# A two-number constant moves from the first SBUF pool to the last: the tiles in between begin 32 bytes lower

## The chip, the core and the metric

The kernel runs on one NeuronCore of a Trainium2 chip. The metric is the device time of one execution in microseconds (us), taken as the median of several executions. SBUF is the core's on-chip memory: 128 partitions, in each of which a tile takes a run of bytes; an address below is the byte within a partition at which a tile begins. Engines are named as in the profile: PE is TensorE's matmul and PEld its weight load, DVE is VectorE, ACT is ScalarE, POOL is GpSimd, SP is the queue that issues most DMAs.

## The reference

A backbone of two layers over 256 latent tokens and 256 context tokens of width 1024. Cut to what the kernel's time goes into:

```python
for l in range(2):
    m = silu(c) @ w_ada[l] + b_ada[l]               # shift, scale, gate: 9 x 1024, for latent and context
    x = ffn_sublayer(x, m, 0, ff1_gate[l], ff1_up[l], ff1_down[l], ...)   # 1024 -> 2816 -> 1024
    y = hybrid_mixer(modulate(x, m, 1), w_in[l], w_out[l], ...)           # attention, RG-LRU, Fourier
    x = layer_norm(alpha * x + m[5] * y)
    x = ffn_sublayer(x, m, 2, ff2_gate[l], ff2_up[l], ff2_down[l], ...)

def ffn_sublayer(x, m, j, wg, wu, wd, g, b):
    h = x * (1 + m[3*j + 1]) + m[3*j]
    y = 0.5 * (silu(h @ wg) * (h @ wu)) @ wd
    return layer_norm(alpha * x + m[3*j + 2] * y)
```

The context stream leaves out what the last layer doesn't need. All inputs and the output are 32-bit floats.

## The kernel before

Activations lie transposed: 8 chunks of 128 features in the partitions, 512 tokens (256 context, 256 latent) along the free dimension. Every large product is done in three passes for accuracy. A weight unit of 128x1024 floats comes by one DMA from SP into a tile `raw` (`issue`, lines 246 to 257), ACT rounds it to fp32r in `whi` (L274), and DVE or POOL writes the rest, raw minus whi, to `wlo` (`split_lo`, L591). The input is split the same way into `hH` and `hL` (for the down projection `aH` and `aL`), and `mmh` (L391) issues high by high, high by low and low by high, each in pieces of 128 weight columns and 256 tokens. Each such matmul has its own weight load of 128x128 from whi or wlo; hH, hL, aH or aL is what moves through the array. In the profile's rows the moving operand stands first: `gu<-hH,whi` reads hH as moving operand and whi as weights. For the transposes (`ptp<-cs,P`) the tile that is transposed (P) is the one that is loaded as weights, and the identity in `cs` moves.

The modulation products go another way: blocks of w_ada come into `raw` too, and DVE multiplies and adds them into `acc` (L302, L304, L298).

SBUF is shared out by pools, in the order in which they are opened, lines 70 to 77: `const` (one copy of each of its tiles), `wraw` (5 tiles `raw`), `whi` (5), `wlo` (5), `acc` (6), `scr` (13 tiles of 512 floats), `sm`, `dv` (small columns). Within a pool the tiles follow each other in the order of their first use, each rounded up to 32 bytes. In `const` come first `xT`, `hH`, `hL`, `aH`, `aL`, then `cs`, `vT`, `onesD`, `one_c`, `pick`, `scol`, and then `join`, the tile that the change moves: 2 floats in each partition. Behind it in `const` stand `bmean`, `kcol`, `lbd`, `fbd`, `AB` and `mcol`. `join` is written once by a DVE reduction at the start and read as the small moving operand of 40 matmuls (`adat<-join,rows`, L332).

What runs in which order is written out by hand and by lists in the kernel; none of it depends on an address.

Of the kernel before, what the change touches and what calls it, by code (L numbers as in the profile page):

```python
# [11 lines left out]
F32 = mybir.dt.float32  # L12
# [53 lines left out]
def kernel(ctx: ExitStack, tc: tile.TileContext, x, cx, vecs, cst, bias, w_ada,  # L66
# [3 lines left out]
    const = ctx.enter_context(tc.tile_pool(name="const", bufs=1))  # L70
# [6 lines left out]
    dv = ctx.enter_context(tc.tile_pool(name="dv", bufs=2))  # L77
# [19 lines left out]
    one_c = const.tile([128, 1], F32, name="one_c")  # L97
    pick = const.tile([128, 2, 2], F32, name="pick")
    scol = const.tile([128, KD, 2], F32, name="scol")
    join = const.tile([128, 2], F32, name="join")  # L100
    bmean = const.tile([128, 6], F32, name="bmean")
    kcol = const.tile([128, 8], F32, name="kcol")
    lbd = const.tile([128, 8, 128], F32, name="lbd")
# [1307 lines left out]
```

## Time and profile before

| | |
|---|---|
| median of 3 runs | 1831.57 us (1828.18 to 1833.34) |
| the profiled execution | 1830.9 us |
| its span, first to last instruction | 1829.0 us |
| mean granted TensorE clock | 0.983 of full speed |
| PE busy | 1751.4 us, 96% of the span, 14241 matmuls |
| DVE busy | 1224.8 us, 67% |
| ACT busy | 700.6 us, 38% |
| POOL busy | 327.9 us, 18% |
| DMA | 253.33 MB, mean 139 GB/s |

A share of busy time is a mean over the whole span. What decides the time is the chain of work that ended last, which the profile follows back from the last instruction.

### The profile page before, as it was taken

The numbers are of one execution on the slowest core, as the hardware profiler recorded it, in microseconds if no ns is written. First come the engines' busy times: TensorE is split into PE (matmuls) and PEld (weight loads), VectorE is DVE, ScalarE is ACT, GpSimd is POOL, SyncE is SP. The second block draws the span as 40 slices with busy tenths as digits, with TensorE's granted clock in tenths as the row PEclk, the third lists the DMA queues.
The fourth block names the chain that finished last, engine by engine and source line by source line (L and its number), as shares of the span: only waits on it lengthen the run. The fifth ranks groups of instructions, "written<-read, shape, count | busy, mean of one in ns | idle before, by whom it ended". The sixth has DMA issues, their size and how long they took to land.

```text
span 1829.0 us, 33865 instructions
## 1 busy us (share of the span) xinstructions
PE 1751.4 (96%) x14241; PEld 1698.2 (93%) x14241; DVE 1224.8 (67%) x1867; ACT 700.6 (38%) x1119; POOL 327.9 (18%) x258
## 2 busy tenths in 40 slices
PE   7999999999899999999999999999999988979997
PEld 5999999998788999999999999999999868869997
DVE  3799899837586488755664569844643759666555
ACT  2232222225756564312222363222222565555443
POOL 0142122215441061000000140000000545140000
PEclk9999999999999999999999999999999999989998
DMA  7566555532223226544453226555653233266662
GB/s 263 181 195 187 170 167 170 171 95 81 69 59 93 59 82 180 162 139 136 132 157 114 86 81 196 166 171 166 178 169 88 81 93 93 82 192 192 177 190 80
DMA packets 375080, 253.33 MB, mean 139 GB/s; under 512 B 8144, under 2 KB 336336, under 8 KB 374928
## 3 DMA queue, kind: packets, MB, share of 16 engines
q1 hardware_dynamic: 373856, 248.81, 46.3%
q8 instruction: 112, 1.84, 0.4%
q0 software_dynamic: 1072, 2.36, 0.4%
q14 instruction: 40, 0.33, 0.1%
HBM read 250.09 MB, written 1.05 MB: 137 GB/s over the span
## 4 chain that ended last, share of the span: by engine, by line
PE 79%; DVE 15%; ACT 3%; issue 2%; DMA 0%; POOL 0%; SPq 0%; DVEq 0%; ACTq 0%
PE gu L391 42%; PE dn L391 21%; PE head L391 5%; PE pj L391 3%; PE wo L391 2%; DVE acc L304 2%; PE adat L332 1%; DVE ri L903 1%; DVE wlo L591 1%; PE o L1097 1%; DVE xl L870 1%; DVE s L460 1%; DVE xT L718 1%; DVE s L463 1%; PE adap L315 1%
## 5 line engine op out<-in xcount | busy, mean ns | idle before, releaser
L391 PE MATMUL gu<-hH,whi 128*128 128x256 f32 x2336 | 500.1, 283 | 2.0 <-ACT hH L1262 1.8
L391 PE MATMUL gu<-hH,wlo 128*128 128x256 f32 x2336 | 497.4, 282 | 2.1 <-DVE wlo L591 2.1
L391 PE MATMUL gu<-hL,whi 128*128 128x256 f32 x2336 | 497.6, 282 | 1.2 <-DVE hL L591 1.1
L274 ACT CAST whi<-raw 128x1024 fp32r<-128x1024 f32 (+1 forms) x319 | 318.8, 1024 | 284.3 <-PE dn L391 104.8
L591 POOL TENSOR_TENSOR wlo<-raw,whi 128x1024 fp32r<-128x1024 f32 (+2 forms) x106 | 207.7, 1966 | 1191.3 <-ACT whi L274 1153.7
L391 PEld LDWEIGHTS gu<-hH,whi 128*128 128x128 f32 x2336 | 374.1, 190 | 5.9 <-ACT hH L1262 2.6
L391 PEld LDWEIGHTS gu<-hH,wlo 128*128 128x128 f32 x2336 | 373.9, 190 | 2.6 <-DVE wlo L591 2.6
L391 PEld LDWEIGHTS gu<-hL,whi 128*128 128x128 f32 x2336 | 374.1, 190 | 1.7 <-DVE hL L591 1.7
L591 DVE TENSOR_TENSOR wlo<-raw,whi 128x1024 fp32r<-128x1024 f32 (+1 forms) x245 | 295.5, 1209 | 92.8 <-ACT whi L274 89.5
L391 PE MATMUL dn<-aH,whi 128*128 128x256 f32 x1280 | 286.3, 283 | 0.8 <-DVE xT L718 0.8
L391 PE MATMUL dn<-aH,wlo 128*128 128x256 f32 x1280 | 283.6, 281 | 0.0
L391 PE MATMUL dn<-aL,whi 128*128 128x256 f32 x1280 | 283.6, 281 | 0.0
L304 DVE SCALAR_TENSOR_TENSOR acc<-raw,scol,acc 128x512 f32<-128x512 f32 x337 | 275.2, 864 | 1.0
L731 ACT CAST aH<-pr 128x512 fp32r<-128x512 f32 (+1 forms) x88 | 50.0, 568 | 422.9 <-DVE pr L730 422.9
L391 PEld LDWEIGHTS dn<-aH,whi 128*128 128x128 f32 x1280 | 208.7, 189 | 1.4 <-DVE xT L718 1.2
L391 PEld LDWEIGHTS dn<-aH,wlo 128*128 128x128 f32 x1280 | 208.7, 189 | 0.1
L391 PEld LDWEIGHTS dn<-aL,whi 128*128 128x128 f32 x1280 | 208.7, 189 | 0.0
L730 DVE TENSOR_TENSOR pr<-sg,gu 128x512 f32<-128x512 f32 (+1 forms) x84 | 51.5, 614 | 148.7 <-PE gu L391 146.2
L718 DVE SCALAR_TENSOR_TENSOR xT<-dn,gate,xT 128x256 f32<-128x256 f32 x174 | 78.0, 478 | 90.5 <-PE dn L391 90.0
L729 ACT ACTIVATE sg<-gu 128x512 f32<-128x512 f32 (+1 forms) x84 | 45.3, 539 | 115.5 <-PE gu L391 115.3
L391 PE MATMUL pj<-hH,whi 128*128 128x256 f32 x384 | 84.5, 288 | 4.9 <-DVE k L591 2.7
L391 PE MATMUL pj<-hH,wlo 128*128 128x256 f32 x384 | 83.1, 285 | 0.0
(239 smaller groups left out, 2127.7 us busy)
## 6 DMA issues: line engine op xcount, KB each, us to landing
raw<-in_w_ada_dram SPq DMA_DIRECT2D x136, 512.0 KB, 4.6
raw<-in_ff_gate_dram SPq DMA_DIRECT2D x88, 512.0 KB, 4.4
raw<-in_ff_up_dram SPq DMA_DIRECT2D x88, 512.0 KB, 4.8
raw<-in_ff_down_dram SPq DMA_DIRECT2D x64, 448.0 KB, 4.5
raw<-in_w_in_dram SPq DMA_DIRECT2D x36, 512.0 KB, 3.9
raw<-in_ff_down_dram SPq DMA_DIRECT2D x32, 512.0 KB, 4.8
raw<-in_w_out_dram SPq DMA_DIRECT2D x16, 512.0 KB, 4.1
in<-in_w_ada_dram SPq DMA_DIRECT2D x8, 512.0 KB, 6.9
```

Source lines behind the costliest of these rows:

```text
L274: S.copy(h_[:, :n], t[:, :n])
L304: V.scalar_tensor_tensor(out=a[:, st], in0=t[:, kk * 512:(kk + 1) * 512], scalar=sc_, in1=a[:, st], op0=ALU.mult, op1=ALU.add)
L315: PE.matmul(acc[l, b][32 * (k % 4):32 * (k % 4) + 32, :], lhsT=scol_z[:, k, :], rhs=t[:, kk * 512:(kk + 1) * 512], start=(k < 4), stop=(k ...
L332: PE.matmul(tp[:, q * 2:q * 2 + 2], lhsT=a[:, q * 128:(q + 1) * 128], rhs=w, start=True, stop=True)
L391: PE.matmul(o[:, c], lhsT=w, rhs=X[:, k, c], start=first and i == 0, stop=last and i == len(halves) - 1)
L460: (e1 or V).tensor_tensor(out=s1, in0=a, in1=z, op=ALU.add)
L463: (e2 or V).tensor_tensor(out=s2, in0=b, in1=sq, op=ALU.add)
L591: (eng or V).tensor_tensor(out=dst_l, in0=src, in1=dst_h.bitcast(F32), op=ALU.subtract)
L718: V.scalar_tensor_tensor(out=xT[:, j, a:b], in0=ps[:, a:b], scalar=gate[:, st, j:j + 1], in1=xT[:, j, a:b], op0=ALU.mult, op1=ALU.add)
L729: S.activation(out=sg[:, c], in_=gp[:, c], func=AF.Silu)
L730: V.tensor_tensor(out=pr[:, c], in0=sg[:, c], in1=up[:, c], op=ALU.mult)
L731: S.copy(aH[:, m, c], pr[:, c])
```

## The change

One line: `join` is taken from the pool `dv`, the last one, in place of `const`, the first one.

```diff
@@ -97,7 +97,7 @@
     one_c = const.tile([128, 1], F32, name="one_c")
     pick = const.tile([128, 2, 2], F32, name="pick")
     scol = const.tile([128, KD, 2], F32, name="scol")
-    join = const.tile([128, 2], F32, name="join")
+    join = dv.tile([128, 2], F32, tag="join", name="join", bufs=1)
     bmean = const.tile([128, 6], F32, name="bmean")
     kcol = const.tile([128, 8], F32, name="kcol")
     lbd = const.tile([128, 8, 128], F32, name="lbd")
```

No instruction is added, removed or moved: on every engine the two programs have the same instructions in the same order. What differs is where tiles begin, as the two built programs have it:

```
tile            address before (mod 64, mod 256)    address now (mod 64, mod 256)
xT..aL, cs, onesD   16512 .. 105600 (0, 128)        the same
join            106240 (0, 0)                       228032 (0, 192)
lbd             106336 (32, 96)                     106304 (0, 64)
raw, first of 5 114656 (32, 224)                    114624 (0, 192)
whi, first of 5 135136 (32, 224)                    135104 (0, 192)
wlo, first of 5 155616 (32, 224)                    155584 (0, 192)
acc, first of 6 176096 (32, 224)                    176064 (0, 192)
scr, first of 13 200672 (32, 224)                   200640 (0, 192)
dv, from mod on 228064 (32, 224)                    the same
```

The tiles of raw, whi, wlo and acc are 4096 bytes and those of scr 2048 bytes, so all of one pool have the same remainders. Everything from `bmean` to the end of `sm` lies 32 bytes lower; `join` fills the 32 bytes that this leaves ahead of the first tile of `dv`.

## Rows read from the trace of the kernel before

**Rows 1.** The page: busy time and share by engine; granted clock in 40 slices, tenths.

```profile
PE 1751.4 (96%) x14241; PEld 1698.2 (93%) x14241; DVE 1224.8 (67%) x1867; ACT 700.6 (38%) x1119; POOL 327.9 (18%) x258
...
PEclk9999999999999999999999999999999999989998
```

**Rows 2.** The page: the chain that ended last, shares of the span by engine.

```profile
PE 79%; DVE 15%; ACT 3%; issue 2%; DMA 0%; POOL 0%; SPq 0%; DVEq 0%; ACTq 0%
```

**Rows 3.** Groups by line and form, PE and PEld: count | busy us, mean ns | idle before.

```profile
L391 PE MATMUL gu<-hH,whi 128*128 128x256 f32 x2336 | 500.1, 283 | 2.0 <-ACT hH L1262 1.8
...
L391 PEld LDWEIGHTS gu<-hL,whi 128*128 128x128 f32 x2336 | 374.1, 190 | 1.7 <-DVE hL L591 1.7
...
L391 PE MATMUL dn<-aH,whi 128*128 128x256 f32 x1280 | 286.3, 283 | 0.8 <-DVE xT L718 0.8
...
L391 PE MATMUL pj<-hH,whi 128*128 128x256 f32 x384 | 84.5, 288 | 4.9 <-DVE k L591 2.7 <-ACT pt L1066 2.2
...
L391 PE MATMUL head<-hH,whi 128*128 128x256 f32 x256 | 67.2, 295 | 9.2 <-ACT hH L605 8.6 <-ACT hH L603 0.6
...
L391 PE MATMUL wo<-aH,whi 128*128 128x256 f32 x144 | 34.7, 286 | 0.0
```

**Rows 4.** Windows, L391 alone: stretch, us, PE and PEld busy (instructions), clock, DMA, GB/s.

```profile
820.24:876.67 56.43, 56.25 (x480) 56.04 (x478) 1.00 0.46 136
```

**Rows 5.** Timeline, PE, first and last of 16 rows: start, length.

```profile
508.69 0.59 PE L958 MATMUL fy<-cs,fas 128*128 128x256 f32 x2
...
515.17 0.59 PE L959 MATMUL fy<-cs,fas 128*128 128x256 f32 x2
```

**Rows 6.** Groups by line and form, PE and PEld, weights at either remainder.

```profile
L332 PEld LDWEIGHTS adat<-pick,fold 128*128 128x128 f32 x192 | 23.4, 191 | 1.4 <-DVE fold L356 1.1 <-PE dn L391 0.2
...
L1064 PEld LDWEIGHTS ptp<-cs,P 128*128 128x128 f32 x80 | 9.1, 140 | 2.4 <-DVE P L996 2.3
...
L1064 PEld LDWEIGHTS ptp<-cs,xT 128*128 128x128 f32 x48 | 5.4, 140 | 1.6 <-ACT xT L1000 1.0 <-ACT whi L274 0.4
...
L804 PEld LDWEIGHTS fab<-fbd,cs 128*128 128x128 f32 x8 | 1.2, 192 | 0.0
...
L1064 PE MATMUL ptp<-cs,P 128*128 128x128 f32 x80 | 11.4, 274 | 1.8 <-DVE P L996 1.8
...
L1064 PE MATMUL ptp<-cs,xT 128*128 128x128 f32 x48 | 6.7, 275 | 0.7 <-ACT xT L1000 0.7
```

**Rows 7.** Groups by line and form, DVE and ACT, tiles at either remainder.

```profile
L591 DVE TENSOR_TENSOR aL<-pr,aH 128x512 fp32r<-128x512 f32 x66 | 45.0, 685 | 6.3 <-ACT aH L731 6.2
...
L603 ACT CAST hH<-h 128x256 fp32r<-128x256 f32 x63 | 25.6, 406 | 2.0
...
L356 DVE TENSOR_TENSOR fold<-fold 128x512 f32<-128x512 f32 x24 | 16.4, 683 | 0.0
...
L660 ACT CAST whi<-raw 128x256 fp32r<-128x256 f32 x16 | 6.4, 402 | 0.0
```

**Rows 8.** DMA queues in three windows, 1.8:2.69, 12:15, 98.9:102 us: packets, MB, share of 16 engines.

```profile
q1 hardware_dynamic: 389, 0.19, 72.9%
...
q1 hardware_dynamic: 603, 1.17, 104.6%
...
q0 software_dynamic: 143, 0.65, 50.7%
```

**Rows 9.** The chain in order of time: start us, length us, what (one piece).

```profile
3.17 7.05 DMA in<-in_x_dram
```

**Rows 10.** Waits by engine: who waited for whom, us in total, times, longest.

```profile
SPq L254 <- POOL wlo L591: 363.5, 55, 21.4
SPq L254 <- DVE wlo L591: 297.8, 129, 20.1
...
ACT whi L274 <- DMA raw<-in_ff_down_dram: 63.2, 15, 9.1
...
PE gu L391 <- DVE wlo L591: 2.1, 2, 1.6
```

## The prediction

> **What bounds the kernel now.** I read the page first: PE is busy 96% of the span, DVE 67%, ACT 38% and POOL 18%, and the granted clock is at 0.9 of full speed or more, its upper level of 2.4 GHz, in 38 of 40 slices [rows 1]. Then the chain that ended last: PE has 79% of it, DVE 15%, ACT 3%, and transfers round to 0% [rows 2]. The reader is to see that the time is PE's stream of matmuls, with DVE's share where PE waits for normalisation and attention, and that no queue of DMAs sets the pace.
>
> The stream is nearly all of one kind, the three-pass fp32r matmul at L391. Its counts per pass are 2336, 1280, 384, 256 and 144 [rows 3]; three passes of each make 13,200 of the 14,241 matmuls. In a stretch with no gap 480 of them take 56.43 us at a clock of 1.00 [rows 4], so 117.6 ns each; 13,200 at that rate are 1552 us of the 1829.0 us span. Every one of them loads 128x128 weights from whi or wlo, which are tiles that the change shifts, and moves hH, hL, aH or aL, which stay.
>
> **The change part by part.** No instruction comes, goes or moves, so the only thing that can change is how long an instruction or a transfer takes when its tile begins 32 bytes lower: at a multiple of 64 bytes, where it began half-way between two. Each kind has a price from the nearest rows.
>
> *Weight loads and their matmuls.* The trace has the same operation with weights at either place. The transposes of attention load P from a tile 32 bytes off a multiple of 64, and others load from xT, which is on one: 140 ns and 140 ns for the load, 274 and 275 ns for the matmul [rows 6]. The load of `fold` (off) takes 191 ns and that of `cs` in the Fourier product (on) 192 ns [rows 6]. Those are fp32 operations; the fp32r ones read the same 512 bytes from each partition, but they have no row with weights on a multiple of 64, since whi, wlo and the attention's q all lie off one. So the price per fp32r matmul is not shown, only bounded. From above: 256 columns at one per cycle of 2.4 GHz are 106.7 ns (an estimate), and the fp32 passes of fy over 256 columns, 16 rows of two, start every (515.17 - 508.69) / 30 = 0.216 us [rows 5], which is two cycles per column (213.3 ns) and 2 to 3 ns, with weights off a multiple of 64. The fp32r matmul has 117.6 - 106.7 = 10.9 ns over its columns, so if the whole difference between 10.9 and 2 ns were due to the address, the change would give back 8.9 ns x 13,200 = 117 us. From below: nothing excludes a loss, because the moving tiles already begin on a multiple of 64 and now both streams do; the nearest rows, xT loaded while cs moves (both on a multiple of 64) beside P, show 1 ns in 275 [rows 6], which at 13,200 would be 13 us of loss. I take zero: the pairs of rows 6 differ in exactly what the change alters, and the fy rows, whose weights `fas` lie off a multiple of 64, have no more than 3 ns over their columns.
>
> The Trainium skill (TensorE: Matmul & The Clock Gate, section "Back-to-back issue gap") gives columns / 2.4 GHz + 2.5 ns for an isolated warm matmul and says that in a stream both the weight load and the matmul set the spacing; by its first formula 256 columns would be 109.2 ns, by its second statement a longer spacing needs no address. The fy rows agree with the 2.5 ns, the 117.6 ns of rows 4 do not; an ideal spacing would make the sum about 111 us less, and nothing on the page ties the spacing to an address.
>
> *DVE and ACT.* A subtraction with all operands in shifted tiles (fold, 683 ns) takes as long as one with two operands in tiles that stay on a multiple of 64 (aL, 685 ns) [rows 7]; a cast between two shifted tiles takes 402 ns, one from a shifted tile to hH 406 ns [rows 7]. The differences are 0.3% and 1%. On the chain DVE has 15%, or 274 us, and ACT 3%, or 55 us [rows 2]: 0.3% of the one and 1% of the other are 0.8 and 0.5 us, either way. I take zero.
>
> *Transfers into raw, acc and scr.* The share of 16 engines' time divided by the bytes gives the cost of a row of 512 bytes (into scr), of 2048 bytes (into raw) and of 5120 bytes (into cs, on a multiple of 64) [rows 8]: 0.729 x 16 x 0.89 us / 0.19 MB x 512 B = 28.0 ns; 1.046 x 48 us / 1.17 MB x 2048 B = 87.9 ns; 0.507 x 49.6 us / 0.65 MB x 5120 B = 198 ns. The line through the first two (8.0 ns and 0.0390 ns per byte) gives 208 ns for the third, so a row that begins on a multiple of 64 is at most 5% cheaper than the line says, and part of that is the rounding of the MB column. Where would it matter? The chain has one long piece of transfer, the 7.05 us until the inputs are there [rows 9]. Later, the queue waits for DVE and POOL to free tiles, 297.8 and 363.5 us [rows 10], not the other way round; ACT waits for transfers, 63.2 us for the down weights [rows 10], but PE's own wait for wlo adds up to 2.1 us [rows 10], so the five tiles of each pool cover it. 5% of 7.05 + 2.1 us is 0.5 us; without that cover, 5% of the 63.2 us would be 3.2 us. I take zero.
>
> The Trainium skill has a rule that speaks here (DMA: Bandwidth & Descriptors, section "How a descriptor splits into AXI transactions"): a transaction starts at a multiple of 256 bytes, and a descriptor that starts elsewhere pays for the bytes ahead of it, in beats of 32 bytes. It speaks of reads; read for the SBUF side, 512 bytes from remainder 224 are 23 beats, and from 192 they are 22. By it the sum would be some 0.4 us lower (4.3% of 9.2 us), by the line of rows 8 at most 0.5 us. Rows 8 neither need the rule nor exclude it.
>
> **The sum.** 1830.9 us (profiled execution) + 0 = 1830.9 us, which is 0.7 us below the median of the runs shown; the forecast is 1831 us. What a measurement of this kernel can tell from no change is about 0.3%, or 5.5 us, since its three runs lie within 1828.2 to 1833.3 us. Over 13,200 matmuls that is 0.42 ns, one cycle of TensorE's clock for each: below that an effect on PE isn't seen, above it it is.
>
> **The rivals.**
>
> *Faster, by the weight loads.* The surplus of 10.9 ns per fp32r matmul comes in part from weights that begin half-way between two multiples of 64. For it: no fp32r row with other weights exists, and fp32 passes have only 2 ns. Against it: rows 6, and that the surplus may as well belong to fp32r itself. One to two cycles per matmul give 5.5 to 11 us: 1820 to 1825 us. All of it gives 1831 - 117 = 1714 us.
>
> *Slower, by two streams in step.* Weights and moving operand now begin at the same remainder by 64 and are read at the same time, every 117.6 ns; if both then ask for the same part of SBUF in the same cycle, one waits. The place is the L391 stream, the price one cycle or more per matmul, and it decides from 0.42 ns on: 1 ns gives 13 us, 1844 us; one cycle 1836.5 us. Against it: the transposes of xT have both operands in step and take what those of P take [rows 6].
>
> *A transfer gets cheaper and nothing follows.* Rows of 512 bytes into raw go from 28.0 to about 27 ns, DMA is 46% busy in the middle stretch [rows 4] and falls by a couple of hundredths, and the time stays within 1 us of 1831 us, since transfers are off the chain. This is "no change" with another trace.
>
> *The tiles don't shift.* If the 32 bytes were lost in padding, nothing would change at all. The address table excludes it: raw goes from 114656 to 114624.
>
> **How the numbers follow.** No measurable change, 1825.5 to 1836.5 us, has 0.77 (of it 0.12 with cheaper transfers). Faster has 0.14: 0.09 for one to two cycles, 0.05 for more than that. Slower has 0.09: 0.05 up to 1840 us, 0.04 beyond. These are the chances of the three verdicts as well. The range reaches into the small cases on both sides: 1822 to 1838 us holds the 0.77, about 0.05 of the faster and 0.02 of the slower; its ends are 0.7 and 0.5 ns per matmul.
>
> **What the changed kernel's profile would show.** If I am right, 480 matmuls of L391 in a gapless stretch again take 56.2 to 56.7 us; the mean load stays at 190 ns [rows 3]; fold and whi keep 683 and 402 ns within 1%; the three DMA shares stay; and the span is 1824 to 1834 us. If the weight loads gain, the 480 take 0.2 us less for each cycle, in all stretches alike. If the streams collide, they take that much longer. If the transfers gain, the share of q1 for the same number of 512-byte packets falls from 72.9% to about 70% with the span unmoved. What would make the prediction wrong is an address that matters to fp32r alone, at the one place where no row of this trace has a pair.

## The result, and the profile after

The changed kernel takes 1809.14 us (median of 4, 1805.85 to 1810.58) where the kernel before, run beside it, takes 1832.29 us: a ratio of 0.9875, 95% interval 0.9855 to 0.9896. It is 23 us faster; the prediction said no change. The profiled execution took 1805.85 us with a span of 1804.1 us, 24.9 us below the span before.

The page after, with the chain's shares, answers to [rows 1, 2]:

```profile
PE 1722.3 (95%) x14241; PEld 1667.0 (92%) x14241; DVE 1227.6 (68%) x1867; ACT 699.9 (39%) x1119; POOL 324.7 (18%) x258
...
PE 76%; DVE 16%; ACT 4%; issue 3%; DMA 0%; POOL 0%; SPq 0%; DVEq 0%; ACTq 0%
```

With the same 14241 matmuls PE is busy 1751.4 - 1722.3 = 29.1 us less. The span fell by 24.9 us, so some 4 us of that came back as idle time of PE, and the chain's shares of DVE, ACT and issue each grew by a point. The busy time of the other engines moved by 1% at most. The groups by line and form (count | busy us, mean ns of one) answer to [rows 3, 6, 7]:

```profile
L391 PEld LDWEIGHTS gu<-hL,whi 128*128 128x128 f32 x2336 | 370.8, 190 | 1.6 <-DVE hL L591 1.6
...
L591 DVE TENSOR_TENSOR aL<-pr,aH 128x512 fp32r<-128x512 f32 x66 | 45.0, 686 | 6.3 <-ACT aH L731 6.2
...
L603 ACT CAST hH<-h 128x256 fp32r<-128x256 f32 x63 | 25.6, 407 | 2.0
...
L356 DVE TENSOR_TENSOR fold<-fold 128x512 f32<-128x512 f32 x24 | 16.4, 682 | 0.0
...
L660 ACT CAST whi<-raw 128x256 fp32r<-128x256 f32 x16 | 6.4, 402 | 0.0
```

DVE's and ACT's means moved by 1 ns at most, and even the mean length of a weight load stands at 190 ns. The queue q1 between 12 and 15 us, packets, MB, share of 16 engines, answers to the second of [rows 8]; transfers cost what they did:

```profile
q1 hardware_dynamic: 599, 1.16, 104.7%
```

What changed is how far apart PE's matmuls of L391 start. The windows, L391 alone (stretch, us, PE and PEld busy with their counts, clock, DMA, GB/s), the last row being the stretch of [rows 4]:

```profile
189.09:234.42 45.33, 45.33 (x384) 45.12 (x384) 1.00 0.53 155
235.21:257.08 21.87, 21.87 (x192) 21.67 (x192) 1.00 0.58 172
333.76:366.51 32.75, 32.75 (x288) 32.55 (x288) 1.00 0.56 160
...
810.52:867.20 56.68, 56.52 (x480) 56.31 (x479) 1.00 0.45 135
```

All four are without gaps and at a granted clock of 1.00, the level of 2.4 GHz, and yet they fall into two kinds. 45.33/384 and 56.64/480 (the chain below) are 118.0 ns per matmul; 21.87/192 and 32.75/288 are 113.9 and 113.7 ns. A stretch has some 0.11 us that does not depend on its count, so differences are cleaner: (45.33 - 22.72) / 192 = 117.8 ns between two slow stretches, (43.63 - 21.87) / 192 = 113.3 ns between two fast ones. The chain of the changed kernel in order of time (start, length, what), in pieces:

```profile
188.30 0.79 PE adat L332 x8
189.09 45.33 PE gu L391 x384
234.42 0.79 PE adat L332 x8
235.21 21.87 PE gu L391 x192
...
367.29 22.72 PE gu L391 x192
...
441.83 18.62 PE head L391 x158
...
619.28 20.00 PE wo L391 x168
...
810.40 56.64 PE gu L391 x480
...
953.43 43.63 PE gu L391 x384
...
1434.77 18.74 PE head L391 x159
...
1564.43 2.74 PE wo L391 x24
...
1791.70 1.41 DVE bn L524 x4
```

The same pieces in the chain of the kernel before, with one more at the head:

```profile
337.52 34.28 PE gu L391 x288
...
449.15 18.55 PE head L391 x158
...
626.56 19.92 PE wo L391 x168
...
820.06 56.43 PE gu L391 x480
...
964.20 45.68 PE gu L391 x384
...
1454.27 18.89 PE head L391 x159
...
1583.44 2.85 PE wo L391 x24
...
1816.66 1.40 DVE bn L524 x4
```

The lead is therefore 7.3 us at the first `head`, 7.3 at the first `wo`, 9.7 and 10.8 in the feed-forward stretches behind it, 19.5 at the later `head`, 19.0 at its `wo` and 25.0 at the end. From `head` to `wo` runs the mixer, 177.4 us before and 177.5 now in the one layer, 129.2 and 129.7 in the other: nothing is gained there, the lead grows in the feed-forward streams. And not in all of their stretches: the x384 stretch at 953 us took 45.68 us before and takes 43.63 us now, the x480 stretch took 56.43 us and takes 56.64 us.

Over all starts of one L391 matmul to the next in stretches without a gap, the trace of the changed kernel has a mean of 115.72 ns and that of the kernel before 118.11 ns. The difference of 2.39 ns on 13,200 matmuls is 31.5 us of stream; three quarters of it or a little more reached the end.

### The profile page after: what moved, and what is told of

The parts are those of the page before. It is cut to its first block, busy times and chain, and to the rows that moved or that the text cites. A ratio compares the mean times of both kernels' runs of the same rounds, so it can differ in the third digit from the quotient of the medians.

```text
span 1804.1 us, 33865 instructions
## 1 busy us (share of the span) xinstructions
PE 1722.3 (95%) x14241; PEld 1667.0 (92%) x14241; DVE 1227.6 (68%) x1867; ACT 699.9 (39%) x1119; POOL 324.7 (18%) x258
## 4 chain that ended last, share of the span: by engine, by line
PE 76%; DVE 16%; ACT 4%; issue 3%; DMA 0%; POOL 0%; SPq 0%; DVEq 0%; ACTq 0%
PE gu L391 41%; PE dn L391 19%; PE head L391 5%; PE pj L391 3%; DVE acc L304 2%; PE wo L391 2%; PE adat L332 1%; DVE wlo L591 1%; DVE ri L903 1%; PE o L1097 1%; DVE xT L718 1%; DVE s L460 1%; DVE xl L870 1%; DVE fold L298 1%; ACT whi L274 1%
## 5 line engine op out<-in xcount | busy, mean ns | idle before, releaser
L391 PE MATMUL gu<-hH,whi 128*128 128x256 f32 x2336 | 494.7, 281 | 1.8 <-ACT hH L1262 1.8
L391 PE MATMUL gu<-hH,wlo 128*128 128x256 f32 x2336 | 491.7, 280 | 1.7 <-DVE wlo L591 1.7
L391 PE MATMUL gu<-hL,whi 128*128 128x256 f32 x2336 | 492.1, 280 | 1.0 <-DVE hL L591 0.9
L391 PEld LDWEIGHTS gu<-hH,whi 128*128 128x128 f32 x2336 | 371.9, 190 | 5.7 <-ACT hH L1262 2.4
L391 PEld LDWEIGHTS gu<-hL,whi 128*128 128x128 f32 x2336 | 370.8, 190 | 1.6 <-DVE hL L591 1.6
L391 PEld LDWEIGHTS gu<-hH,wlo 128*128 128x128 f32 x2336 | 370.0, 189 | 2.2 <-DVE wlo L591 2.2
L391 PE MATMUL dn<-aH,whi 128*128 128x256 f32 x1280 | 283.5, 281 | 1.6 <-DVE xT L718 1.6
L391 PE MATMUL dn<-aL,whi 128*128 128x256 f32 x1280 | 281.0, 279 | 0.0
L391 PE MATMUL dn<-aH,wlo 128*128 128x256 f32 x1280 | 280.8, 279 | 0.0
L391 PEld LDWEIGHTS dn<-aH,whi 128*128 128x128 f32 x1280 | 207.5, 189 | 2.1 <-DVE xT L718 2.0
L391 PEld LDWEIGHTS dn<-aL,whi 128*128 128x128 f32 x1280 | 207.7, 189 | 0.0
L391 PEld LDWEIGHTS dn<-aH,wlo 128*128 128x128 f32 x1280 | 207.1, 188 | 0.1
L391 PE MATMUL pj<-hH,whi 128*128 128x256 f32 x384 | 84.0, 287 | 5.5 <-ACT pt L1066 2.8
L391 PE MATMUL pj<-hH,wlo 128*128 128x256 f32 x384 | 82.7, 283 | 0.0
```

What stands on the lines that cost most here:

```text
L391: PE.matmul(o[:, c], lhsT=w, rhs=X[:, k, c], start=first and i == 0, stop=last and i == len(halves) - 1)
```

## The experiments

Rivals at the start: **A**, the weights' own place counts (a multiple of 64 is fast); **B**, fast when weights and moving operand have the same remainder by 64; **C**, it comes from transfers, or from DVE, ACT and POOL tiles. Later **D**: what counts is the distance from the moving tile's start to the weights' start, by some period. Slices of L391 are 512 bytes in the weights and 1024 or 2048 bytes in the moving tiles, so by a period of 512 or less every matmul of a kernel has the same distance; it was 352 bytes before and is 320 bytes now (remainder by 512). The "mean spacing" below is the mean start to start as above.

**w_only** shifts whi and wlo of the kernel before 32 bytes up, to a multiple of 256 (distance 384). acc and what lies behind it go up by 64 bytes and stay 32 off a multiple of 64:

```diff
+    pad_whi = ctx.enter_context(tc.tile_pool(name="pad_whi", bufs=1))
+    pad_whi.tile([128, 8], F32, name="pad_whi_t")
     (and the same ahead of acc)
```

> The kernel before, with a pad of 32 bytes ahead of the whi pool and another behind the wlo pool: whi and wlo begin on a multiple of 64 bytes, raw stays 32 off, acc and scr stay 32 off, join stays in const. Theory A (the place of the weights themselves sets the spacing of the fp32r matmuls): about 1809 us, spacing in two levels near 113.3 and 117.8 ns. Theory B (it is weights and moving operand having the same remainder by 64): the same, 1809 us. Theory C (transfers into raw, or DVE, ACT and POOL on raw, acc and scr): 1832 us, spacing 117.3 and 118.7 ns.

Measured 1837.42 us, ratio 1.004 (1.0026 to 1.0053); mean spacing 118.69 ns. Weights on a multiple of 64 are not fast by themselves: A falls, and B with it, since the moving tiles start on one too.

**rest_only** makes the same edit in the changed kernel, so that whi and wlo are back at their old place, raw keeps the new one, acc and scr stay on a multiple of 64, and `join` stays in `dv`.

```diff
+    pad_whi = ctx.enter_context(tc.tile_pool(name="pad_whi", bufs=1))
+    pad_whi.tile([128, 8], F32, name="pad_whi_t")
     (and the same ahead of acc)
```

> The changed kernel, with the same two pads: raw, lbd, acc and scr begin on a multiple of 64, whi and wlo 32 off. Theories A and B: about 1832 us, spacing 117.3 and 118.7 ns as before the change. Theory C: about 1809 us.

Measured 1830.08 us, ratio 1.0001 (0.9991 to 1.0011), 117.85 ns; its x480 stretch takes what it took before the change (the pads move line 391 to 395):

```profile
816.77 56.43 PE gu L395 x480
```

Without whi and wlo nothing is left of the gain. C falls, and so does the move of `join` itself as a cause.

**both_32** shifts everything in the changed kernel up by 32 bytes, moving operands and weights alike (distance 320 as in the changed kernel, both off a multiple of 64):

```diff
+    const.tile([128, 8], F32, name="pad_c")
     xT = const.tile(...)
```

> The changed kernel with a pad of 32 bytes as the first tile of const: every tile of the matmuls, moving (hH, hL, aH, aL) and weights (whi, wlo), begins 32 off a multiple of 64, so both have the same remainder. Theory A (weights alone): about 1832 us or somewhat more, if the moving operand has a price of its own. Theory B (same remainder): about 1809 us.

Measured 1806.86 us, ratio 0.9879 (0.9857 to 0.9901), 115.51 ns. The chain of both_32 and then that of w_only, start, length, what:

```profile
809.16 54.51 PE gu L392 x480
...
948.83 45.33 PE gu L392 x384
```

```profile
822.77 57.06 PE gu L395 x480
...
967.85 45.67 PE gu L395 x384
```

In both_32 the x480 stretch is a fast one, (54.51 - 0.11) / 480 = 113.3 ns, and the x384 stretch a slow one, 117.8 ns: the two levels of the changed kernel in other stretches. In w_only there is one level, 118.7 ns. So neither place counts alone, but the two together.

**plus32** reaches w_only's distance of 384 by another edit, 32 bytes more in `const` of the kernel before:

```diff
     join = const.tile([128, 2], F32, name="join")
+    const.tile([128, 8], F32, name="pad_j")
```

> The kernel before with a pad of 32 bytes behind join in const: join stays where it was and all pools behind it begin 32 bytes higher, not lower, on a multiple of 64 (and here of 256). Theories A and B: about 1809 us. If it were join's own move to the last pool, or the remainder by 256 of 192: 1832 us.

Measured 1838.53 us, ratio 1.0042 (1.0029 to 1.0055), 118.70 ns, as w_only.

**move64, move96, move128, move160** leave the weights where they were before and shift xT, hH, hL, aH and aL up, by placing small tiles of `const` ahead of them instead of behind (cs, vT and onesD go up with them). Distances 288, 256, 224 and 192.

```diff
+    scol = const.tile([128, KD, 2], F32, name="scol")      (move64 and on)
+    pick = const.tile([128, 2, 2], F32, name="pick")       (move96 and on)
+    one_c = const.tile([128, 1], F32, name="one_c")        (move128 and on)
+    bmean = const.tile([128, 6], F32, name="bmean")        (move160)
     xT = const.tile(...)
```

> The kernel before with scol as the first tile of const: xT, hH, hL, aH, aL, cs, vT and onesD begin 64 bytes higher, all pools behind const stay. The distance from the moving operand to the weights is then 32 mod 128 (288 mod 512), a remainder not yet seen. Theory D (the distance decides, by its remainder by 128: 64 fast, 96 as before, 0 slow): a value of its own; between the kernel before and the changed one, some 1810 to 1830 us, if the slow remainder is 0 and the fast one 64. Theory A (weights' own place): 1832 us.

> The kernel before with scol and pick as the first tiles of const: moving tiles 96 bytes higher, distance 0 mod 128 and 0 mod 256 (256 mod 512), where the two slow runs had 128 mod 256. Theory D with 128 as the period: about 1838 us, spacing 118.7 ns throughout. Theory D with 256: another time. Theory A: 1832 us.

> The kernel before with scol, pick and one_c as the first tiles of const: moving tiles 128 bytes higher, distance 96 mod 128 as before the change (224 mod 256, where the kernel before has 96). Theory D with 128 as the period: about 1831 us, spacing 117.3 and 118.7 ns. With 256: another time. Theory A: 1832 us.

> The kernel before with scol, pick, one_c and bmean as the first tiles of const: moving tiles 160 bytes higher and 32 off a multiple of 64, weights unmoved and 32 off; distance 64 mod 128 as in the changed kernel (192 mod 256, where that has 64). Theory D with 128 as the period: about 1808 us, spacing 113.3 and 117.8 ns. With 256: another time. Theory A: 1832 us.

Measured 1833.62, 1851.77, 1818.26 and 1826.4 us, ratios 1.0015 (1.0006 to 1.0025), 1.0116 (1.0099 to 1.0132), 0.9938 (0.9924 to 0.9953) and 0.9977 (0.9968 to 0.9987). move96 makes the kernel 21 us slower without moving its weights. From its chain:

```profile
827.70 57.70 PE gu L391 x480
```

Every stretch of it has 120.0 ns, (57.70 - 0.11) / 480. A period of 128 is excluded: 256 and 384 bytes would be the same then, and 352 and 224 too, but they take 1852 and 1838 us, and 1831 and 1818 us.

**dist64 and dist160** ask whether the period is 256: 64 should be as 320, and 160 is a distance not seen yet.

```diff
     (dist64: mcol, scol, pick, one_c, bmean ahead of xT)
     (dist160: scol, pick, one_c, bmean, kcol ahead of xT)
```

> The kernel before with mcol (2 tiles of 576 bytes), scol, pick, one_c and bmean as the first tiles of const: the moving tiles begin 1312 bytes higher, weights unmoved; distance 64 mod 512, where the changed kernel has 320. Theory D with 256 as the period (320 and 64 alike): about 1808 us, spacing 113.3 and 117.8 ns. With 512: another time, any between 1800 and 1852 us.

> The kernel before with scol, pick, one_c, bmean and kcol as the first tiles of const: moving tiles 192 bytes higher, weights unmoved; distance 160 mod 256, the one remainder by 256 not yet seen. Theory D gives no number for it, but a spacing of its own that holds in every stretch of the stream, between 113 and 120 ns, so 1795 to 1852 us; theory A (weights' own place): 1832 us.

Measured 1820.82 us, 0.9939 (0.9922 to 0.9956), and 1849.98 us, 1.0101 (1.0086 to 1.0117). dist64 has the two levels of 320, but only 18% of its matmuls stand on the fast one where the changed kernel has near half. The chain of dist64:

```profile
190.74 43.64 PE gu L391 x384
...
816.04 56.64 PE gu L391 x480
```

So the levels speak for 256, and something else decides which level a stretch gets. In the trace a level holds from break to break, in one kernel for 1313 matmuls, and a break that can change it is the short group of fp32 matmuls `adat`. Counted over such breaks, changed kernel: fast to slow 13 of 13, slow to fast 15 of 18; dist64: slow to slow 26 of 28. (In the rows such a group is `x8`: four matmuls of fp32, two records each. So the 40 records of `join` are 20 matmuls.)

**L1** has the break decide the level; **L2** has the period be 512, with 64 another distance than 320. **dist64_pick** is dist64 with `pick`, the break's moving operand, at the changed kernel's distance from `fold` and whi, 32 by 256 (160 in dist64):

```diff
     (scol, pick, mcol, one_c, bmean ahead of xT)
```

> dist64 (distance 64 mod 512) with pick, the small moving operand of the adat matmuls that break the stream, further ahead in const, so that its distance to fold and whi is 32 mod 256 as in the changed kernel (in dist64 it was 160). Theory L1 (which of the two levels a stretch takes up is left over from the break, and the distance inside the break sets it): the levels 113.3 and 117.8 ns alternate over about half the stream each, 1808 us. Theory L2 (512 is the period, and 64 differs from 320): 1821 us as dist64, with 113.3 ns in about a fifth.

**pick_32** is the reverse, the changed kernel with pick at 160:

```diff
-    pick = const.tile([128, 2, 2], F32, name="pick")
     ...
     kcol = const.tile([128, 8], F32, name="kcol")
+    pick = const.tile([128, 2, 2], F32, name="pick")
```

> The changed kernel with pick behind kcol in const: pick at distance 160 from fold and whi as in dist64, nothing else moves but scol, bmean and kcol by at most 32 bytes; hH, hL, aH, aL, whi and wlo stay. L1: about 1821 us, with 117.8 ns in most stretches behind an adat break. L2: 1808 us as the changed kernel.

Measured 1806.79 us, 0.9865 (0.9845 to 0.9885), and 1822.33 us, 0.9952 (0.9937 to 0.9968). One small tile that the short breaks read moves 13 to 14 us either way (mcol and the tiles between change their place with it). The chains of dist64_pick and of pick_32:

```profile
810.78 56.64 PE gu L391 x480
...
953.82 43.63 PE gu L391 x384
```

```profile
334.52 0.79 PE adat L332 x8
335.31 34.03 PE gu L391 x288
...
370.12 22.72 PE gu L391 x192
...
959.17 45.33 PE gu L391 x384
```

dist64_pick alternates as the changed kernel does (15 of 15, 15 of 16); pick_32 stays slow (25 of 27). The breaks last 0.79 us in either, so they cost the same; they differ in what they leave behind. pick's distance to hH changes along with that to fold, so which of the two counts isn't shown. With the break's distance equal, 64 and 320 are alike in levels and time.

**wlo_back and low_back** put one third of the passes at another distance: the changed kernel with wlo at 352, and with hL and aL at 288. **D1** has the passes' spacings average, **D2** has the worst one hold the rest.

```diff
+    pad_wlo = ctx.enter_context(tc.tile_pool(name="pad_wlo", bufs=1))
+    pad_wlo.tile([128, 8], F32, name="pad_wlo_t")
     (low_back: const in the order hH, aH, one_c, hL, aL)
```

> The changed kernel with a pad of 32 bytes ahead of the wlo pool: whi keeps the distance of the changed kernel (320 mod 512), wlo gets that of before (352). Of six weight loads in a round two are of wlo. Theory D1 (each load and the matmul beside it make a pair, and the pairs' prices add up): 1809 + 1/3 x 22 = about 1816 us, with the longer spacing at the matmuls beside loads of wlo. Theory D2 (one bad distance spoils the whole stream's step): 1831 us or more.

> The changed kernel with the tiles in the order hH, aH, one_c, hL, aL: hL and aL begin 32 bytes further, at distance 288 from both weights, hH and aH keep 320. Two of six matmuls in a round move hL or aL. D1 (pairs add up): 1809 + 1/3 x (1834 - 1809) = about 1817 us, the longer spacing at the hL and aL matmuls. D2: 1834 us or more.

Measured 1829.62 us, 0.9994 (0.9985 to 1.0004), 117.95 ns, and 1821.45 us, 0.9944 (0.9928 to 0.9959), 117.25 ns. The time of the first came out near D2's, that of the second between the two. But in wlo_back the time goes where D1 has it, beside the loads of wlo. Rows of its timeline, two matmuls each (start, length, what):

```profile
826.11 0.40 PE L393 MATMUL gu<-hH,whi 128*128 128x256 f32 x2
826.34 0.41 PE L393 MATMUL gu<-hH,wlo 128*128 128x256 f32 x2
826.59 0.39 PE L393 MATMUL gu<-hL,whi 128*128 128x256 f32 x2
```

From the start of the pair with wlo to the next pair it is 0.25 us, from the pair ahead of it 0.23 us. So neither theory holds as it stands. In wlo_back acc moves with wlo, so the break's distance from pick to fold changes too, from 32 to 64.

**adat_5, adat_6 and adat_split** ask whether a break can be made to lead into the fast level. The first two repeat the last of the break's four products once or twice (the same result written again), the third splits the last product in two halves, which leaves the work the same.

```diff
-        for q in range(4):
+        for q in (0, 1, 2, 3) + (3,) * 1:                  (adat_5; * 2 in adat_6)
```

```diff
-        for q in range(4):
+        for q, r in ((0, (0, 128)), (1, (0, 128)), (2, (0, 128)), (3, (0, 64)), (3, (64, 128))):
             (PE.matmul on the rows r[0]:r[1] of product q)
```

> The changed kernel with the last of the four matmuls of each adat break done twice (the same numbers written again): 36 breaks longer by 2 records of about 0.111 us, 8 us in all if the stream is else as it was, so 1817 us. L1 (the break's length and reads set the level behind it): the alternation of 113.3 and 117.8 ns changes; if each break then leads into the same level as before it, either 117.8 throughout, 1840 us, or 113.3 throughout, about 1790 us. L3 (the level has nothing to do with the break): half and half as before, 1817 us.

> The changed kernel with the last of the four matmuls of each adat break done three times: 36 breaks longer by 4 records, 16 us if the stream is else as it was, so 1825 us. L1: the levels behind the breaks change against adat_5; 1798 to 1848 us. L3: 1825 us, half and half.

> The changed kernel with the last of the four matmuls of each adat break split in two halves of 64 weight columns: five matmuls in a break, as in adat_5, but no more columns loaded than before. If what flips the level is the number of matmuls in the break (theory L1 with parity), 113.3 ns follows 113.3 ns as in adat_5 and the 8 us of extra loads are saved: about 1795 us. If it is the break's length in time, the alternation stays: 1809 us. If a half load counts otherwise, anything from 1785 to 1840 us.

Measured 1803.28 us (1795.5 to 1815.09), 0.9872 (0.9822 to 0.9923); 1824.39 us, 0.997 (0.9958 to 0.9982); and 1801.14 us (1788.98 to 1806.67, 6 runs), 0.9825 (0.98 to 0.985). The chains of adat_5 and of adat_split:

```profile
189.01 1.01 PE adat L332 x10
190.02 43.63 PE gu L391 x384
...
234.66 21.87 PE gu L391 x192
...
810.47 54.51 PE gu L391 x480
```

```profile
188.48 0.78 PE adat L332 x10
189.25 43.73 PE gu L392 x384
...
332.14 34.12 PE gu L392 x288
...
367.03 22.81 PE gu L392 x192
```

With a fifth matmul the break keeps a fast stream fast (25 of 26), and in the profiled execution, one of 1797.25 us, 75% of the matmuls are on the fast level, mean spacing 114.49 ns; but each break is 0.22 us longer, and the median is no better than the changed kernel's by more than the intervals tell. With a sixth it alternates again (15 of 18, 13 of 14). adat_split carries either level over (14 of 15, 14 of 16) at no cost, and its runs spread over 18 us, perhaps by the level with which each starts, which isn't shown. Its median is the lowest found, and its interval lies below the changed kernel's, though not below that of adat_5.

All kernels by distance (remainder by 512, in brackets by 256). "Levels" are spacings within stretches:

| kernel | distance | levels, ns | mean, ns | median, us |
|---|---|---|---|---|
| move96 | 256 (0) | 120.00 | 119.96 | 1851.77 |
| move64 | 288 (32) | 118.33 | 118.33 | 1833.62 |
| changed | 320 (64) | 113.33, 117.78 | 115.72 | 1809.14 |
| both_32 | 320 (64) | 113.33, 117.78 | 115.51 | 1806.86 |
| dist64_pick | 64 (64) | 113.33, 117.78 | 115.54 | 1806.79 |
| dist64 | 64 (64) | 113.33, 117.78 | 117.00 | 1820.82 |
| before | 352 (96) | 117.33, 118.67 | 118.11 | 1831.57 |
| rest_only | 352 (96) | 117.33, 118.67 | 117.85 | 1830.08 |
| w_only, plus32 | 384 (128) | 118.67 | 118.7 | 1837.42, 1838.53 |
| dist160 | 160 (160) | 120.00 | 119.98 | 1849.98 |
| move160 | 192 (192) | 113.33 (4%), 117.78 | 117.61 | 1826.4 |
| move128 | 224 (224) | 116.67, 117.78 | 117.01 | 1818.26 |

The break's distance from pick to fold differs among these kernels (by 256: 32 in the changed one, both_32, dist64_pick, dist160 and move96 to move160; 64 before; 0 in move64; 160 in dist64). Where a kernel has two levels, its mean therefore belongs to the stream and the break together; the levels are the same in dist64 and dist64_pick, which differ in the break.

The time follows the mean spacing: from move96 to the changed kernel 42.6 us for 4.24 ns, 10 us per ns, where 13,200 matmuls would make it 13.2.

## Why the prediction was wrong

**The bound.** Right: the time is PE's stream at L391, no queue sets the pace, and whatever touches this stream touches the end.

**Weight loads and their matmuls.** This is the step that failed. The prediction bounded the price from 0 to 117 us of gain, with some loss below, and took zero because "the pairs of rows 6 differ in exactly what the change alters". They do differ in the variable that turned out to count: cs moves in both and stays, so P lies 96 bytes from it by 256 and xT 0, and that step is worth 1.9 ns to the fp32r stream (before, 118.11 ns; move96, 119.96). But they are fp32 matmuls of two passes, and those don't show it. The fy rows tell it best: the change takes `fas` from a distance of 96 to 64 from the moving cs, as it takes whi from hH. In the changed kernel, second and last of the 16 rows:

```profile
502.64 0.59 PE L959 MATMUL fy<-cs,fas 128*128 128x256 f32 x2
...
508.68 0.59 PE L959 MATMUL fy<-cs,fas 128*128 128x256 f32 x2
```

That is (508.68 - 502.64) / 28 = 0.216 us from start to start, as before the change and as in move96, where the distance is 0. Measured for the fp32r matmul: 2.39 ns each, 31.5 us of stream, 23 us of time, and no gain from the weights' own place (w_only, both_32). The bounds held; the choice between ends far apart was made by rows of another operand type, and their zero was carried over. The last sentence of the prediction names just this as what would make it wrong, an address that matters to fp32r alone; it was given 0.23 of the chances, both ways together.

**DVE, ACT and transfers at zero.** Right, by the rows after and by rest_only, which has no gain left.

**The rival "faster, by the weight loads"** came nearest in time, 1820 to 1825 us for one to two cycles, but its mechanism is not what the runs show: multiples of 64 are as good or bad as others. The mean gain was 5.7 cycles.

**The rival "slower, two streams in step"** had both streams in it, and the wrong rule. With both on a multiple of 64 the spacing is 113.3 or 117.8 ns at a distance of 320, and 118.7 ns at 384. That it ended on the gaining side could not be seen from the kernel before, which has one distance only.

**The sign to look for.** One sign of being right was that 480 matmuls again take 56.2 to 56.7 us. They take 56.64 us, because that stretch got the slow level, while others fell by 4 to 5% (x288 from 34.28 to 32.75 us). A check on one stretch of a stream that has two levels tells nothing; "in all stretches alike" was the assumption. The sign that did tell was the span, 1804.1 us where 1824 to 1834 was forecast.

**Where the rest of the gain went.** Of 31.5 us of stream some 25 us reached the end of the profiled execution. PE's own waits grew by some 4 us in all, most at `adat` for DVE's fold (1.0 to 3.0 us) and at `gate` for xl (7.4 to 8.9 us); what else took part of the gain was not followed up.

The Trainium skill (TensorE: Matmul & The Clock Gate, section "Step-by-step: what each phase is for") says that the weight load and the moving operand have read ports of their own and that loading the next weights takes no read bandwidth from the running matmul. In these runs the two are not independent: the same instructions at the same clock take 1807 to 1852 us by how these two operands lie to each other. Whether it is read bandwidth that they compete for, no run shows.

## What to carry to other kernels

In a kernel bound by a long stream of fp32r matmuls, each with its own weight load, treat the distance between the weights' tile and the moving tile as a parameter, worth 2.5% between its worst and its best here, and try it in steps of 32 bytes over 256: a pad or a small tile moved is the whole edit, and 64 by 256 was the best here. The operands of short breaks in the stream belong to the same search, at 13 to 14 us here. Judge it by the mean start to start over all stretches, because a stretch can stand on either of two levels. When the rows that vary the address are of another kind of matmul, their agreement is no reason to take zero: leave the range open as far as the bounds go.

## What the hardware showed that was not expected

The stream's spacing has memory. Two stretches with the same instructions, distance and clock run at 113.3 or 117.8 ns per matmul from their first to their last, and the level before and the short break between decide which: the break's operand's distance (dist64_pick and pick_32, 13 to 14 us) and its number of matmuls (adat_5, mean 114.49 ns). The stream's own distance matters too: in move160, with the changed kernel's break distance, a slow stretch stays slow (32 of 32).

The levels are odd in a regular way. In cycles of 2.4 GHz 113.33 ns are 272 = 17 x 16 and 120.0 ns are 288 = 18 x 16, and the others come to whole multiples of 16 over two to five matmuls: 116.67 x 2 = 560, 117.78 x 3 = 848, 118.33 x 4 = 1136, 118.67 x 5 = 1424 and 117.33 x 5 = 1408 cycles. That looks like a stream that slips by 16 cycles at a time, an estimate from the spacings alone; what meets what in SBUF no run shows.

It also stays open whether the period is 256 at every distance (only 64 and 320 were compared), how the three passes' distances combine (wlo_back and low_back), why fp32 doesn't show the effect, and whether a break exists that always leads into the fast level at no cost; steps finer than 32 bytes were not tried. The fp32 matmuls kept their spacing where the distance of their operands changed: `fy` 216 ns in both kernels and in move96.
